# A hybrid attention block on one core: all engines in written order through the attention stages, score masks between normalisation steps, decay rows prepared amid the value projection

## The chip, the cores and the metric

The kernel runs on one core of a Trainium2 chip. The metric is device time in microseconds. The core's engines are TensorE (PE in the profile, with its weight loads as PEld), VectorE (DVE), ScalarE (ACT), GpSimd (POOL) and SyncE (SP), which here issues nearly all DMAs. Each engine takes its own instructions strictly in the order in which they stand; engines wait for each other on semaphores.

## The reference

One layer of a decoder block. Two attentions read the same normalised input, one with low-rank queries and keys (MLA), one with a forget gate (FoX); each has 16 heads of 64 and 512 tokens behind 16 learned ones. Their gated outputs are merged.

```python
u = rmsnorm(h, pre_norm_g[l])
proj = u @ w_in[l]
(cq, ckv, k_pe_raw, z_mla, fq, fk, fv, f_logit, z_fox, gate_a, gate_b) = jnp.split(proj, split_idx, axis=-1)
q = (rmsnorm(cq, mla_q_norm_g[l]) @ w_uq[l])...
kv = (rmsnorm(ckv, mla_kv_norm_g[l]) @ w_ukv[l])...
o_mla = causal_block_attention(q_m, k_m, v_mla, MLA_SCALE)
y_mla = (o_mla * jax.nn.silu(z_mla)) @ w_br_mla[l]
log_f = jax.nn.log_sigmoid((f_logit + fox_forget_b[l]).astype(jnp.float32)).transpose(0, 2, 1)
cum = jnp.cumsum(log_f, axis=-1)
o_fox = causal_block_attention(fox_heads(fq), fox_heads(fk), fox_heads(fv), FOX_SCALE, cum)
y_fox = (o_fox * jax.nn.silu(z_fox)) @ w_br_fox[l]
mixed = (jax.nn.sigmoid(gate_a) * y_mla + jax.nn.sigmoid(gate_b) * y_fox) @ w_out[l]
h = h + rmsnorm(mixed, post_norm_g[l])
```

In the FoX branch a logit gets `cum[t] - cum[s]`; the term of the query falls out of the softmax, so the kernel adds only a row over the keys.

## The kernel before

Float32 operands are split into a high and a low part, and a product is three matmuls (high by high, high by low, low by high). A weight tile is loaded as `wraw` (line 132, SP), cast to `wh` on ScalarE (line 141), and its rest `wl` is formed on GpSimd or VectorE (line 117).

After an opening, 16 attention stages run, one for each pair of heads and branch: `stages` takes FoX, then MLA, for pairs 0 to 7. A stage has these steps.

- Scores: `scores(0)` for query blocks 0 to 2, `scores(1)` for block 3. TensorE writes them to four rotating PSUM banks (`st`). VectorE adds the mask row, keeps the running minimum for the softmax (line 925), and so frees the bank. In MLA the row is `maskt`; in FoX it is `cdiag` (the decay with the causal mask in it) for the diagonal block, and for keys before it a copy of the plain decay in the last tile of `gT`.
- Exponentials (line 935, ScalarE), reciprocals of the sums (944, 945, VectorE), normalised probabilities as a high half (963, ScalarE) and a low half (964, VectorE), the 16 learned tokens' on GpSimd (950 to 955), and DMA transposes `pt<-pn` on SP (971), eight for a stage.
- `values()`: the product `ov` of a stage's probabilities and values. It is run one stage later, on TensorE between the two groups of scores.
- `fill`: the projections for the next stage and for the gates, between and behind the steps above. In a FoX stage these are `z` (both gates), MLA's `mq`, `mk` and `v`; in an MLA stage FoX's `fq`, `fk` and `v`, 48 matmuls each for `fk` and `v`. Pair 1's MLA stage also has the second half of the rotary queries (`ppe`). The keys' and queries' halves are written by `hl_done` (266 on ScalarE, 117 on VectorE). For `v` VectorE finds the peak of each half (805), then a power of two (810 to 815), and ScalarE scales (825).

A FoX stage's decay rows take three steps. `load_diag` brings `c_dram` into `cdiag`, a row of 528 numbers spread over 128 partitions for each of two heads (line 285, two DMAs). `keep_off` copies the part before the diagonal into `gT` (289, ScalarE). `mask_diag` adds the causal mask to `cdiag` in place (294, VectorE).

What sets the order: in the first stage every engine's instructions stand as the code is written. From the second on only TensorE's do; for the other four a scheduler orders them by priority, with `tc.high_priority` around masks, exponentials and casts. `load_diag` is called in an MLA stage and `keep_off` and `mask_diag` when `fk` is done, but the scheduler moves them, as the rows below show.

Of the kernel before, what the change touches and what calls it, by code (L numbers as in the profile page):

```python
# [14 lines left out]
BF16 = mybir.dt.bfloat16  # L15
# [8 lines left out]
S = 512  # L24
META = 16
# [29 lines left out]
def block_kernel(ctx: ExitStack, tc: tile.TileContext, x, meta_tokens, pre_norm_g, w_in, fox_forget_b,  # L55
# [238 lines left out]
        nc.vector.tensor_tensor(out=d, in0=d, in1=m, op=ALU.add)  # L294

    def k_fox(pr, put=None):
        halves = hl_done(("k", 1, pr), L, HALF, put)

        def done(i, ps):
            halves(i, ps)  # L300
            if pr and i:
                keep_off()
                mask_diag()
        return unit(f"fk{pr}", win_w(O_FK, pr), u_act, KD, ALLT, done)

# [360 lines left out]
    with ExitStack() as att:  # L668
# [45 lines left out]
        def q_mla(pr):  # L714
            kv = wukv.rearrange("p (h a e) -> p a h e", a=2, e=HD)

            def wrap(w):
                mw[pr] = w
                return (lambda k: w[k][0]), (lambda k: w[k][1])
            get = weights(lambda: [wuqh[:, k, 2 * pr : 2 * pr + 2, 0:NOPE] for k in range(2)]  # L720
                          + [kv[:, i, 2 * pr : 2 * pr + 2, :] for i in range(2)], wrap)

            halves = hl_done(("q", 0, pr), S, S)

            def q_done(i, ps):
                halves(i, ps)
                if pr:
                    load_qp(pr)
            return unit(f"mq{pr}", get, cq_act, 2, REAL, q_done)

# [142 lines left out]
        def attention(br, pr):  # L875
# [28 lines left out]
            def scores(g):  # L904

                banks = (((0, 0, 144, 0), (1, 0, 272, 144)), ((2, 0, 400, 0),)) if g == 0 else \
                    (((3, 0, HALF, 0),), ((3, HALF, L - HALF, 0),))

                def fn():
                    if g == 0:  # L910
                        for t in ("nb", "su", "ri"):
                            sums[t] = aw.tile([128, 2, 4], F32, tag=t, name=f"{t}{nm_}")
                    sfs[g] = aw.tile([128, 2, (2 * SF_STEP + 400, L)[g]], F32, tag=f"sf{g}", name=f"sf{nm_}{g}", bufs=1)
                    for ib, parts in enumerate(banks):
                        ps = [stp.tile([128, 512], F32, tag="st", name=f"st{nm_}{g}{ib}{h}") for h in range(2)]
                        for b, c0, w, o in parts:
                            for i, ops in enumerate(zip(*(sets(h, b, c0, w) for h in range(2)))):
                                for h, (Q, K) in enumerate(ops):
                                    mm(ps[h][:, o : o + w], Q, K, start=(i == 0), stop=(i == 4 - 2 * br))
                        for b, c0, w, o in parts:  # L920
                            for h in range(2):
                                nb = sums["nb"][:, h, b : b + 1]
                                for c1, n, add in terms(h, b, c0, w):
                                    with tc.high_priority(offset=100):
                                        nc.vector.tensor_tensor_reduce(  # L925
                                            out=sf_of(h, b)[:, c1 : c1 + n], in0=ps[h][:, o + c1 - c0 : o + c1 - c0 + n],
                                            in1=add, scale=-scale, scalar=3.0e38 if c1 == 0 else nb,
                                            op0=ALU.add, op1=ALU.min, accum_out=nb)

                def ex(mid={}):  # L930
                    with tc.high_priority(offset=60):
                        for b in GRP[g]:
                            for h in range(2):
                                sf = sf_of(h, b)
                                nc.scalar.activation(sf, sf, AF.Exp, bias=sums["nb"][:, h, b : b + 1], scale=-1.0,  # L935
                                                     accum_out=sums["su"][:, h, b : b + 1])
                                mid.get((b, h), int)()
                return fn, ex

            def norm(g):  # L940
                def fn(mid=int):
                    b0, nb_ = GRP[g][0], len(GRP[g])
                    su, ri = (sums[t][:, :, b0 : b0 + nb_] for t in ("su", "ri"))
                    nc.vector.tensor_scalar(out=su, in0=su, scalar1=1.0 / PSCALE, scalar2=None, op0=ALU.mult)
# [8 lines left out]
                    nc.gpsimd.tensor_copy(hi, mt)  # L953
                    nc.gpsimd.tensor_tensor(out=lo, in0=mt, in1=hi, op=ALU.subtract)
                    nc.gpsimd.tensor_copy(hi2, mt)
                    for b in GRP[g]:
                        for h in range(2):
                            sf = sf_of(h, b)[:, META:].rearrange("p (j c) -> p j c", c=128)
                            t0 = PN_STEP * (b % 3) + 1
                            hi, lo = (pn[g][:, h, t0 : t0 + 2 * b + 2].rearrange("p (j l) c -> p j l c", l=2)[:, :, i]  # L960
                                      for i in range(2))
                            rib = sums["ri"][:, h, b : b + 1]
                            nc.scalar.activation(hi, sf, AF.Copy, scale=rib)  # L963
                            nc.vector.scalar_tensor_tensor(out=lo, in0=sf, scalar=rib, in1=hi, op0=ALU.mult,  # L964
                                                           op1=ALU.subtract)
                    for b in GRP[g]:
                        if b == 1:
                            mid()
                        for h in range(2):
                            t0 = PN_STEP * (b % 3)  # L970
                            nc.sync.dma_start_transpose(
                                out=pts[h][:, 0 : 2 * b + 3, 128 * b : 128 * b + 128],
                                in_=pn[g][:, h, t0 : t0 + 2 * b + 3].rearrange("p t c -> p (t c)"))
                return fn

            def values():
                po = ovp.tile([128, 512], F32, tag="ov", name=f"ov{nm_}")
# [3 lines left out]
                for j in range(4):  # L981
                    for i, (v, p) in enumerate(((0, 0), (0, 1), (1, 0))):
                        for h in range(2):
                            mm(ph[h][:, 128 * j :], vps[br][:, j, h, v], pts[h][:, 1 + 2 * j + p, 128 * j :], start=False,
                               stop=(j == 3 and i == 2))
                nc.vector.scalar_tensor_tensor(out=gT[br][:, pr, :], in0=po, scalar=vsc[br, pr], in1=sils[br, pr],
                                               op0=ALU.mult, op1=ALU.mult)
                if br and pr % 2:
                    g2 = gT[1][:, pr - 1 : pr + 1].rearrange("p k s -> p (k s)")
                    sumsq(g2, gss[:, 1, pr // 2 : pr // 2 + 1], sils[1, pr].bitcast(BF16))  # L990

            return scores(0), scores(1), norm(0), norm(1), values

# [4 lines left out]
        def feed(br, pr):  # L998

            q = (q_mla, q_fox)[br](pr)  # L1000
            k = (k_mla, k_fox)[br](pr)
            v, vts[br, pr] = v_unit(br, pr, put=(br, pr) == (0, 0))
            return q, k, v

        def ahead(steps):
# [48 lines left out]
            for name in LAST:  # L1054
                later[name]()
        pe, pe_turn, pe_rest, _ = pe_unit(1)
        fills[3][25:25] = pe + [(0, pe_turn)] + [(0, lambda x=x: pe_rest(x)) for x in (1, 0)]
        steps = sum(fills[1:], []) + tail + mgates[0].steps
        ahead(steps)
        nxt = [fn for _, fn in steps if hasattr(fn, "load")]  # L1060
        late = []
        for si, (br, pr) in enumerate(stages):
            (s0, e0), (s1, e1), n0, n1, va = attention(br, pr)

            fill = fills[si]
            with ExitStack() as head:
                if si == 0:
                    head.enter_context(tc.manual_schedule(engines={E_.PE, E_.SP, E_.Pool, E_.Activation, E_.DVE}))
                    s0()
                    e0()  # L1070
                    run(fill[:3])
                    lo("b")()
                    nxt[1].load()
                    nxt[2].load()
                    n0()
                    s1()
                    run(fill[3:8])
                    e1()
                    run(fill[9:11])
                    run(fill[8:9])  # L1080
                    n1()
                    for x in (1, 0):
                        for i in range(2):
                            rope0[2](i, x, 2)
                    run(fill[11:18])
                    nxt[0].make()
                    run(fill[18:22])
                    for name in ("vr0", "vr1", "vs", "vz"):
                        later[name]()
                    nxt[1].make()  # L1090
                    run(fill[22:])
                    later["vT"]()
                    nxt[2].make()
                else:
                    s0()
                    e0()
                    for fn in late:
                        fn()
                    s1()
                    e1()  # L1100
                    if br == 0 and pr + 1 < NH // 2:
                        load_diag(pr + 1)
                    run(fill[:4])
                    n0()
                    run(fill[4:11])
                    n1()
                    run(fill[11:])
            late = [va]
        run(tail[:4])
        mgates[0].make()  # L1110
        for g in mgates[1:3]:
            g.load()
        va()
        run(tail[4:])


    fctx.close()
# [372 lines left out]
```

## Time and profile before

| | us |
|---|---|
| median of three runs | 621.31 (620.94 to 621.5) |
| the profiled execution | 621.72 |
| its span, first to last instruction | 619.9 |

The page gives the busy time of each engine over the span; the list of waits says for whom an engine stood idle, with the total, the count and the longest; a window gives busy times within a stretch; the timeline gives instructions in order of time, with the idle time before them in brackets. The granted clock of TensorE is 0.997 over the span.

### The profile page before, as it was taken

What the parts mean: (1) busy time and instruction counts of PE and PEld (TensorE: products, weight loads), DVE (VectorE), ACT (ScalarE), POOL (GpSimd) and SP (SyncE); (2) the same over time, 40 slices, a digit from 0 to 9 for tenths busy, and PEclk for the clock granted to TensorE, in tenths of its full rate; (3) what the DMA queues carried; (4) which work ended last, traced back from release to release, by engine and by line L of the source; (5) the groups of instructions that cost most, each with busy time, mean ns of one, the idle gap of its engine ahead of it and who ended that gap; (6) DMA issues with size and microseconds to landing.
All of it is one profiled execution on the core that took longest, in us unless ns stands there. A gap on an engine that the chain in (4) does not pass through costs nothing. (4 is left out here: it accounts for less than half of the span.)

```text
span 619.9 us, 11591 instructions
## 1 busy us (share of the span) xinstructions
PE 603.1 (97%) x3986; PEld 490.9 (79%) x3986; DVE 408.9 (66%) x1129; ACT 389.0 (63%) x855; POOL 176.5 (28%) x227
## 2 busy tenths in 40 slices
PE   9999969999999999999999999999999999999996
PEld 5889759879879879879779788787888875565885
DVE  5948755686675874884874874766977865556134
ACT  7756856676775874874794784776767654444421
POOL 2002444344653353444343353420000000003700
PEclk9999999999999999999999999999999999999999
DMA  9514569876777478476587666677252137332202
GB/s 305 127 39 133 145 149 182 182 178 158 213 153 182 127 170 181 104 180 161 146 161 144 164 152 156 127 176 219 62 152 83 35 88 251 102 106 100 102 35 102
DMA packets 206790, 88.85 MB, mean 143 GB/s; under 512 B 122858, under 2 KB 197994, under 8 KB 206731
## 3 DMA queue, kind: packets, MB, share of 16 engines
q1 hardware_dynamic: 206728, 88.11, 55.8%
q8 instruction: 31, 0.51, 0.3%
q14 instruction: 29, 0.23, 0.2%
q10 hardware_dynamic: 2, 0.00, 0.0%
HBM read 58.69 MB, written 3.97 MB: 101 GB/s over the span
## 5 line engine op out<-in xcount | busy, mean ns | idle before, releaser
L117 POOL TENSOR_TENSOR wl<-wraw,wh 128x1024 fp32r<-128x1024 f32 (+1 forms) x54 | 119.4, 2214 | 276.1 <-ACT wh L141 264.2
L141 ACT CAST wh<-wraw 128x1024 fp32r<-128x1024 f32 (+1 forms) x74 | 72.9, 987 | 83.9 <-issue 34.4
L935 ACT ACTIVATE sf<-sf,nb 128x272 f32<-128x272 f32 (+3 forms) x128 | 72.0, 570 | 10.4 <-DVE nb L925 10.3
L964 DVE SCALAR_TENSOR_TENSOR pn<-sf,ri,pn 128x128 f16<-128x128 f32 (+3 forms) x128 | 65.8, 554 | 2.9 <-ACT pn L963 2.5
L963 ACT ACTIVATE pn<-sf,ri 128x128 f16<-128x128 f32 (+3 forms) x128 | 61.8, 550 | 6.6 <-ACT sf L935 4.1
L91 PE MATMUL pg<-uTh,wh 128*128 128x512 f32 x128 | 51.9, 406 | 0.0
L91 PE MATMUL z<-uTh,wh 128*128 128x512 f32 x128 | 51.1, 400 | 0.0
L91 PE MATMUL z<-uTl,wh 128*128 128x512 f32 x128 | 50.1, 391 | 0.0
L91 PE MATMUL z<-uTh,wl 128*128 128x512 f32 x128 | 50.0, 391 | 0.0
L91 PE MATMUL pg<-uTh,wl 128*128 128x512 f32 x128 | 50.0, 391 | 0.0
L91 PE MATMUL pg<-uTl,wh 128*128 128x512 f32 x128 | 49.8, 389 | 0.0
L91 PE MATMUL st<-hlk,hlq 64*128 64x272 f32 (+3 forms) x480 | 47.8, 312 | 0.0
L91 PE MATMUL py<-g,yw 128*128 128x512 f16 x192 | 42.6, 379 | 0.6 <-DVE yw L1253 0.6
L91 PEld LDWEIGHTS st<-hlk,hlq 64*128 64x128 f32 x480 | 35.6, 188 | 7.2 <-issue 3.8
L91 PE MATMUL fk<-uTh,wh 128*128 128x256 f32 (+1 forms) x128 | 36.6, 286 | 0.0
L91 PE MATMUL v<-uTh,wh 128*128 128x256 f32 (+1 forms) x128 | 36.5, 285 | 0.0
L91 PE MATMUL fk<-uTh,wl 128*128 128x256 f32 (+1 forms) x128 | 36.5, 285 | 0.0
L91 PE MATMUL fk<-uTl,wh 128*128 128x256 f32 (+1 forms) x128 | 36.4, 285 | 0.0
L91 PE MATMUL v<-uTl,wh 128*128 128x256 f32 (+1 forms) x128 | 36.4, 285 | 0.0
L91 PE MATMUL v<-uTh,wl 128*128 128x256 f32 (+1 forms) x128 | 36.4, 285 | 0.0
L91 PEld LDWEIGHTS <-yw 128*128 128x128 f16 x192 | 17.9, 98 | 22.7 <-DVE yw L1253 1.1
L805 DVE TENSOR_REDUCE vsc<-v 128x1 f32<-128x272 f32 (+1 forms) x32 | 13.2, 433 | 33.3 <-PE v L91 33.3
(303 smaller groups left out, 1556.9 us busy)
## 6 DMA issues: line engine op xcount, KB each, us to landing
wraw<-in_w_in_dram SPq DMA_DIRECT2D x56, 512.0 KB, 3.6
cdiag<-c_dram SPq DMA_DIRECT2D x16, 264.0 KB, 4.8
yraw<-in_w_br_fox_dram SPq DMA_DIRECT2D x8, 512.0 KB, 3.8
yraw<-in_w_br_mla_dram SPq DMA_DIRECT2D x8, 512.0 KB
wraw<-in_w_out_dram SPq DMA_DIRECT2D x8, 512.0 KB, 4.8
pt<-pn SPq DMA_TRANSPOSE x128, 2.8
xr<-in_x_dram SPq DMA_DIRECT2D x4, 512.0 KB
out_dram<-yo SPq DMA_DIRECT2D x8, 256.0 KB, 2.1
```

The source lines that it names most:

```text
L91: nc.tensor.matmul(*a, **k)
L117: eng.tensor_tensor(out=lo, in0=src, in1=f32(hi), op=ALU.subtract)
L141: nc.scalar.copy(wh[:, :n], raw[:, :n])
L805: nc.vector.tensor_reduce(out=st["sc"][:, i : i + 1], in_=ps, op=ALU.max, axis=AX.X, apply_absolute_value=True)
L935: nc.scalar.activation(sf, sf, AF.Exp, bias=sums["nb"][:, h, b : b + 1], scale=-1.0, accum_out=sums["su"][:, h, b : b + 1])
L963: nc.scalar.activation(hi, sf, AF.Copy, scale=rib)
L964: nc.vector.scalar_tensor_tensor(out=lo, in0=sf, scalar=rib, in1=hi, op0=ALU.mult, op1=ALU.subtract)
```

## The change

All five engines now follow the written order through all 16 stages. TensorE's own order is the same, instruction by instruction. The score function is split in two, `products` (TensorE) and `masks` (VectorE, a few at a time); the normalisation in three, `sums_`, `halves` (one block and head) and `turn` (its transpose); `values()` returns its gating product and its squares, to be called later. Weight splits (`make`), the small steps of `v` and the decay rows are called by name.

```diff
-                def fn():
+                todo = []
+
+                def products():
...
-                                        nc.vector.tensor_tensor_reduce(
...
+                                    todo.append((h, b, c1, n, ps[h][:, o + c1 - c0 : o + c1 - c0 + n], add))
+
+                def masks(count=99):
+                    for h, b, c1, n, ps, add in todo[:count]:
+                        nb = sums["nb"][:, h, b : b + 1]
+                        nc.vector.tensor_tensor_reduce(
...
+                    del todo[:count]
```

The order of a stage behind the first, as it is written now:

```diff
-                    s0()
-                    e0()
-                    for fn in late:
-                        fn()
-                    s1()
-                    e1()
-                    if br == 0 and pr + 1 < NH // 2:
-                        load_diag(pr + 1)
-                    run(fill[:4])
-                    n0()
-                    run(fill[4:11])
-                    n1()
-                    run(fill[11:])
+                s0()
+                m0()
+                e0()
...
+                gated, squares = last()
+                last = values
+                s1()
+                n0()
+                gated()
+                for i, (h, b) in enumerate(first):
+                    h0(h, b)
+                    if i < 2:
+                        m1(2 + br)
+                    if h:
+                        t0(0, b)
+                        t0(1, b)
+                e1()
+                n1()
+                if br:
+                    second()
+                    run(fill[:8])
+                    make()
+                    squares()
+                    run(fill[8:22])
+                    small("vr0", "vr1", "vs", "vz")
+                    make()
+                    run(fill[22:])
+                    small("vT")
+                    make()
+                    continue
+                run(fill[:4])
+                second()
+                squares()
...
+                run(fill[4:9])
+                make()
+                load_qp(pr + 1)
+                load_diag(pr + 1)
+                run(fill[9:25])
+                make()
...
+                v = fill[-16:]
+                run(v[:8])
+                small("vr0")
+                keep_off()
+                mask_diag()
...
+                run(v[8:])
+                small("vr1", "vs", "vz", "vT")
+                make()
```

`k_fox` and `q_mla` lose their calls of `keep_off`, `mask_diag` and `load_qp`, and `v` is written with its small steps apart (`put=True`) in every stage.

First place: SP in the FoX stage of pair 3, before (`cdiag` the next pair's decay rows, `pt<-pn` the transposes):

```order
L132 DMA wraw_2817<-in_w_in_dram 128x8x128
L132 DMA wraw_2847<-in_w_in_dram 128x8x128
L285 DMA cdiag<-c_dram 128x528 x2
L971 DMA_TRANSPOSE pt_624<-pn_622 128x3x128
L971 DMA_TRANSPOSE pt_625<-pn_622 128x3x128
```

The load stands ahead of that stage's transposes; `QP`, MLA's rotary queries, is loaded after the first two transposes of the MLA stage.

SP in the MLA stage of pair 3, after the change:

```order
L960 DMA_TRANSPOSE pt_624<-pn_622 128x7x128
L960 DMA_TRANSPOSE pt_625<-pn_622 128x7x128
L960 DMA_TRANSPOSE pt_624<-pn_623 128x9x128
L960 DMA_TRANSPOSE pt_625<-pn_623 128x9x128
L132 DMA wraw_3121<-in_w_in_dram 128x8x128
L705 DMA QP<-qpe_dram 128x512
L285 DMA cdiag<-c_dram 128x528 x2
L132 DMA wraw_3185<-in_w_in_dram 128x8x128
```

Both loads now stand behind all eight transposes of the MLA stage and behind a weight load.

Second place: VectorE around the mask of the decay rows. Before, it stands in the FoX stage (pair 3), between the low half of MLA's queries and those of its keys:

```order
L117 TENSOR_TENSOR hlq_2826<-mq_2819,hlq_2826 128x512
L294 TENSOR_TENSOR cdiag<-cdiag,maskt 128x2x512
L117 TENSOR_TENSOR hlk_2869<-mk_2865,hlk_2869 128x272
L117 TENSOR_TENSOR hlk_2869<-mk_2872,hlk_2869 128x256
L805 TENSOR_REDUCE vsc_2888<-v_2884 128x1
```

After, it stands in the MLA stage of pair 3, between the peaks of the two halves of `v`; the first masks of the next FoX stage follow:

```order
L792 TENSOR_REDUCE vsc_3212<-v_3187 128x1
L294 TENSOR_TENSOR cdiag<-cdiag,maskt 128x2x512
L792 TENSOR_REDUCE vsc_3212<-v_3217 128x1
L797 TENSOR_SCALAR vsc_3212<-vsc_3212 128x1
L798 TENSOR_SCALAR vsc_3212<-vsc_3212 128x1
L800 TENSOR_SCALAR vsc_3212<-vsc_3212 128x1
L802 RECIPROCAL vsc_3212<-vsc_3212 128x1
L917 ISA sf_3260,nb_3257<-st_3261,cdiag 128x144
```

So everything that VectorE does for the next FoX stage now stands behind the mask, and the mask behind the load of `cdiag`.

More of the change, by code (lines that the diff above doesn't have):

```diff
@@ L296, in k_fox @@
     def k_fox(pr, put=None):
[L297 to L304, printed above, removed]
+        return unit(f"fk{pr}", win_w(O_FK, pr), u_act, KD, ALLT, hl_done(("k", 1, pr), L, HALF, put))
     gctx = [ExitStack(), ExitStack()]
@@ L721, in q_mla @@
                           + [kv[:, i, 2 * pr : 2 * pr + 2, :] for i in range(2)], wrap)
[L723 to L729, printed above, removed]
+            return unit(f"mq{pr}", get, cq_act, 2, REAL, hl_done(("q", 0, pr), S, S))
         def pe_unit(g, get0=None, put=None):
@@ L920, in fn @@
                         for b, c0, w, o in parts:
[L921 to L928, printed above, removed]
+                            for pair in zip(*(terms(h, b, c0, w) for h in range(2))):
+                                for h, (c1, n, add) in enumerate(pair):
+                                    todo.append((h, b, c1, n, ps[h][:, o + c1 - c0 : o + c1 - c0 + n], add))
[3 more added lines that the diff above has]
+                        nc.vector.tensor_tensor_reduce(
+                            out=sf_of(h, b)[:, c1 : c1 + n], in0=ps, in1=add, scale=-scale,
+                            scalar=3.0e38 if c1 == 0 else nb, op0=ALU.add, op1=ALU.min, accum_out=nb)
+                    del todo[:count]
                 def ex(mid={}):
@@ L937, in ex, with sums_ @@
                                 mid.get((b, h), int)()
-                return fn, ex
+                return products, masks, ex
             def norm(g):
-                def fn(mid=int):
+                def sums_():
                     b0, nb_ = GRP[g][0], len(GRP[g])
@@ L955, in fn, with halves, turn @@
                     nc.gpsimd.tensor_copy(hi2, mt)
[L956 to L974, printed above, removed]
+                def halves(h, b):
+                    sf = sf_of(h, b)[:, META:].rearrange("p (j c) -> p j c", c=128)
+                    t0 = PN_STEP * (b % 3) + 1
+                    hi, lo = (pn[g][:, h, t0 : t0 + 2 * b + 2].rearrange("p (j l) c -> p j l c", l=2)[:, :, i]
+                              for i in range(2))
+                    rib = sums["ri"][:, h, b : b + 1]
+                    nc.scalar.activation(hi, sf, AF.Copy, scale=rib)
+                    nc.vector.scalar_tensor_tensor(out=lo, in0=sf, scalar=rib, in1=hi, op0=ALU.mult, op1=ALU.subtract)
+                def turn(h, b):
+                    t0 = PN_STEP * (b % 3)
+                    nc.sync.dma_start_transpose(
+                        out=pts[h][:, 0 : 2 * b + 3, 128 * b : 128 * b + 128],
+                        in_=pn[g][:, h, t0 : t0 + 2 * b + 3].rearrange("p t c -> p (t c)"))
+                return sums_, halves, turn
             def values():
@@ L985, in values, with gated, squares @@
                                stop=(j == 3 and i == 2))
[L986 to L990, printed above, removed]
+                def gated():
+                    nc.vector.scalar_tensor_tensor(out=gT[br][:, pr, :], in0=po, scalar=vsc[br, pr], in1=sils[br, pr],
+                                                   op0=ALU.mult, op1=ALU.mult)
+                def squares():
+                    if br and pr % 2:
+                        g2 = gT[1][:, pr - 1 : pr + 1].rearrange("p k s -> p (k s)")
+                        sumsq(g2, gss[:, 1, pr // 2 : pr // 2 + 1], sils[1, pr].bitcast(BF16))
+                return gated, squares
             return scores(0), scores(1), norm(0), norm(1), values
@@ L1001, in feed @@
             k = (k_mla, k_fox)[br](pr)
-            v, vts[br, pr] = v_unit(br, pr, put=(br, pr) == (0, 0))
+            v, vts[br, pr] = v_unit(br, pr, put=True)
             return q, k, v
@@ L1056, in block_kernel @@
         pe, pe_turn, pe_rest, _ = pe_unit(1)
-        fills[3][25:25] = pe + [(0, pe_turn)] + [(0, lambda x=x: pe_rest(x)) for x in (1, 0)]
+        fills[3][25:25] = pe
         steps = sum(fills[1:], []) + tail + mgates[0].steps
@@ L1060, in block_kernel, with make, small, second @@
         nxt = [fn for _, fn in steps if hasattr(fn, "load")]
[L1061 to L1066, printed above, removed]
+        queue = nxt[3:-1]
+        def make():
+            queue.pop(0).make()
+        def small(*names):
+            for name in names:
+                later[name]()
+        with tc.manual_schedule(engines={E_.PE, E_.SP, E_.Pool, E_.Activation, E_.DVE}):
+            last = None
+            for si, (br, pr) in enumerate(stages):
+                (s0, m0, e0), (s1, m1, e1), (n0, h0, t0), (n1, h1, t1), values = attention(br, pr)
+                fill = fills[si]
+                first = [(h, b) for b in GRP[0] for h in range(2)]
+                def second():
+                    for h in range(2):
+                        h1(h, 3)
+                    for h in range(2):
+                        t1(h, 3)
+                s0()
+                m0()
+                e0()
                 if si == 0:
-                    head.enter_context(tc.manual_schedule(engines={E_.PE, E_.SP, E_.Pool, E_.Activation, E_.DVE}))
-                    s0()
-                    e0()
                     run(fill[:3])
@@ L1075, in block_kernel @@
                     n0()
+                    for h, b in first:
+                        h0(h, b)
+                    for h, b in first:
+                        t0(h, b)
                     s1()
+                    m1()
                     run(fill[3:8])
@@ L1087, in block_kernel @@
                     run(fill[18:22])
-                    for name in ("vr0", "vr1", "vs", "vz"):
-                        later[name]()
+                    small("vr0", "vr1", "vs", "vz")
                     nxt[1].make()
                     run(fill[22:])
-                    later["vT"]()
+                    small("vT")
                     nxt[2].make()
-                else:
-                    s0()
-                    e0()
-                    for fn in late:
-                        fn()
-                    s1()
-                    e1()
-                    if br == 0 and pr + 1 < NH // 2:
-                        load_diag(pr + 1)
-                    run(fill[:4])
-                    n0()
-                    run(fill[4:11])
-                    n1()
-                    run(fill[11:])
@@ L1108, in block_kernel @@
[L1108 to L1114, printed above, removed]
+                    last = values
+                    continue
+                gated, squares = last()
+                last = values
+                s1()
+                n0()
+                gated()
+                for i, (h, b) in enumerate(first):
+                    h0(h, b)
+                    if i < 2:
[3 more added lines that the diff above has]
+                        t0(1, b)
@@ new lines, in block_kernel @@
+                e1()
[6 more added lines that the diff above has]
+                    run(fill[8:22])
+                    small("vr0", "vr1", "vs", "vz")
+                    make()
+                    run(fill[22:])
+                    small("vT")
+                    make()
+                    continue
+                run(fill[:4])
+                second()
+                squares()
@@ new lines, in block_kernel @@
+                if si + 1 == len(stages):
+                    run(fill[4:])
+                    break
+                run(fill[4:9])
[4 more added lines that the diff above has]
+                make()
+                if si == 3:
+                    run(fill[25:29])
+                    pe_turn()
+                    make()
+                v = fill[-16:]
+                run(v[:8])
+                small("vr0")
@@ L1117, in block_kernel @@
+                keep_off()
+                mask_diag()
+                if si == 3:
+                    for x in (1, 0):
+                        pe_rest(x)
+                run(v[8:])
+                small("vr1", "vs", "vz", "vT")
+                make()
+            run(tail[:4])
+            mgates[0].make()
+            for g in mgates[1:3]:
+                g.load()
+            last()[0]()
+            run(tail[4:])
     fctx.close()
```

## The prediction

> **What bounds the kernel now.** First the page's head, then the list of waits on TensorE.
>
> ```profile
> span 619.9 us, 11591 instructions
> ...
> PE 603.1 (97%) x3986; PEld 490.9 (79%) x3986; DVE 408.9 (66%) x1129; ACT 389.0 (63%) x855; POOL 176.5 (28%) x227
> ```
> ```profile
> PE ov L91 <- DMA pt<-pn: 5.0, 4, 3.2
> PE v L91 <- DVE hlk L117: 4.1, 7, 1.0
> ```
> TensorE is busy for 97% of the span and its order is not changed, so the change can only win back its waits in the attention stages, or add new ones. Two waits are listed there: the values' product `ov` for its transposes (5.0), and the value projection `v` for the keys' lower halves (4.1). What they cost with all that hangs on them is read from stage lengths: windows that begin where a stage's scores begin, with length, busy time of PE, PEld, DVE, ACT, POOL, and PE's granted clock.
>
> ```profile
> 82.74:112.36 29.62, 25.80 (x203) 23.02 (x202) 14.19 (x45) 16.27 (x39) 11.71 (x14) 0.94 0.82 175
> ...
> 132.47:158.88 26.41, 26.41 (x215) 23.62 (x214) 15.62 (x48) 17.36 (x42) 15.74 (x18) 1.00 0.74 186
> ...
> 202.88:223.00 20.12, 19.59 (x129) 15.47 (x128) 17.43 (x60) 15.22 (x38) 7.39 (x11) 1.00 0.49 120
> 223.00:246.64 23.64, 23.64 (x203) 21.39 (x202) 13.17 (x44) 15.48 (x39) 10.70 (x13) 1.00 0.81 184
> ...
> 379.47:398.79 19.32, 19.32 (x128) 15.55 (x128) 14.84 (x59) 14.37 (x36) 7.37 (x11) 1.00 0.45 84
> ```
> The stages alternate: forgetting attention (I call it F), then MLA (M), for pairs 0 to 7. F3 takes 20.12; F7, whose `v` doesn't wait, takes 19.32. M3 takes 23.64 with PE never idle; M0 takes 29.62. So M0 has 5.98 to give, and F1 to F6 about 0.80 each.
>
> Why F waits is seen on four engines at one place of F3:
>
> ```profile
> 217.31 0.95 ACT L289 COPY gT<-cdiag 128x400 f32<-128x400 f32 x2
> 218.29 2.68 DVE L294 TENSOR_TENSOR cdiag<-cdiag,maskt 128x1024 f32<-128x1024 f32 x1 [0.73 <-ACT gT L289]
> 220.89 0.76 DVE L117 TENSOR_TENSOR hlk<-mk,hlk 128x272 fp32r<-128x272 f32 x2
> 221.38 0.40 PE L91 MATMUL v<-cTh,wh 128*128 128x272 f32 x1 [0.53 <-DVE hlk L117]
> 217.49 2.40 POOL L117 TENSOR_TENSOR wl<-wraw,wh 128x1024 fp32r<-128x1024 f32 x1 [4.62 <-ACT wh L141]
> ```
> VectorE adds the causal mask to the next pair's decay rows (`cdiag`) for 2.68, and the keys' lower half, for which PE waits, stands behind it. And in M0:
>
> ```profile
> 81.26 1.01 SPq L285 DMA_DIRECT2D cdiag<-c_dram  x2
> 82.37 4.86 SPq L971 DMA_TRANSPOSE pt<-pn  x2
> 87.29 3.65 SPq L784 DMA_DIRECT2D qpe_dram<-gT  x4
> ...
> 86.44 0.52 ACT L289 COPY gT<-cdiag 128x400 f32<-128x400 f32 x1 [5.08 <-DMA cdiag<-c_dram]
> ...
> 87.67 1.22 DVE L294 TENSOR_TENSOR cdiag<-cdiag,maskt 128x1024 f32<-128x1024 f32 x1 [5.09 <-ACT gT L289]
> ...
> 88.27 0.38 PE L91 MATMUL ov<-pt,vm 80*64 80x512 f16 x1 [3.17 <-DMA pt<-pn]
> ```
> The load of `cdiag` goes ahead of F0's last two transposes, ScalarE and VectorE stand for 5 us until it lands, and PE waits 3.17 for the transposes.
>
> **What the change removes.** (1) In M0 the load no longer stands there, so the transposes follow from 81.26 at about 1.24 each; the second lands some 2.8 after its issue at 82.5, thus at 85.3, where `ov` asks at 85.0. I leave 0.3 and take 5.7. (2) In F1 to F6 the mask leaves the place ahead of the keys: 6 x 0.80 = 4.8. (3) The other waits of `ov` are 5.0 less M0's 3.17 and 0.61, that is 1.2. ScalarE now writes probabilities right after the first group's exponentials, not after the second's, so transposes start earlier in F and this goes. Together 11.7. F0's wait at `v` (the 1.0 of the list) stays, since F0 was in written order already.
>
> **What it adds.** The two copies and the mask now stand in M, on VectorE between the peaks of the two halves of `v`, and the load of `cdiag` stands on SP behind M's eight transposes, one weight load and the load of `QP`. In M3, from its start at 223.00:
>
> ```profile
> 223.06 0.53 SPq L132 DMA_DIRECT2D wraw<-in_w_in_dram  x1
> 225.89 1.82 SPq L132 DMA_DIRECT2D wraw<-in_w_uq_dram  x2
> 227.76 0.97 SPq L132 DMA_DIRECT2D wraw<-in_w_ukv_dram  x2
> 228.83 0.41 SPq L132 DMA_DIRECT2D wraw<-in_w_in_dram  x1
> 230.52 2.48 SPq L971 DMA_TRANSPOSE pt<-pn  x2
> 233.09 0.53 SPq L712 DMA_DIRECT2D QP<-qpe_dram  x1
> 233.71 8.65 SPq L971 DMA_TRANSPOSE pt<-pn  x6
> 242.45 1.16 SPq L132 DMA_DIRECT2D wraw<-in_w_in_dram  x2
> ```
> ```profile
> 230.08 0.41 POOL L954 TENSOR_TENSOR pn<-mt,pn 128x96 f16<-128x96 f32 x1
> ```
> ```profile
> L971 SPq DMA_TRANSPOSE pt<-pn x128: 1178/1237/3468, 71.8 to 416.4; - x128
> ```
> ```profile
> DMA to landing us min/median/max: 4.2/4.8/5.2
> ```
> The first transpose goes at 7.5 into the stage, when GpSimd's last piece is there; the work ahead of it (masks, exponentials) keeps its order in M, so it can't go earlier. Eight issues take 2.48 + 8.65; without `QP` between them they end at 18.7. Then a weight load (0.63 with its gap), `QP` (0.62), and the two loads of `cdiag`, the second at 20.4. The last row is that of `cdiag`'s loads (min, median, max): with 4.8 it lands at 25.2. A copy of 0.52 and the mask at 1.22 end at 27.0. VectorE wants to go on earlier:
>
> ```profile
> 243.88 0.44 DVE L805 TENSOR_REDUCE vsc<-v 128x1 f32<-128x272 f32 x1 [1.70 <-PE v L91]
> 246.75 0.42 DVE L805 TENSOR_REDUCE vsc<-v 128x1 f32<-128x256 f32 x1 [2.43 <-PE v L91]
> ```
> The second peak was due at 246.75, 23.75 into the stage. It comes **3.3 late**, and behind it on VectorE stand the scale of `v` and all score masks of the next F. Those free the score banks:
>
> ```profile
> 206.64 0.35 DVE L925 CUSTOM_DVE_ANT_0 sf<-st,cdiag,nb 128x128 f32<-128x128 f32 x1
> ...
> 206.30 1.38 PE L91 MATMUL st<-hlk,hlq 64*128 64x272 f32 x12
> ```
> In F3 the last mask of the first group ended at 206.92, while PE was within the second group's scores, whose last bank takes that buffer. There is no slack, so PE waits about as long as VectorE is late, in each F from F1 to F7.
>
> The sum: F3 to F7 5 x 3.3 = 16.5. M1 is 26.41 long, 2.77 more than M3, since it holds the second half of the rotary queries, so F2 waits only 0.5. In M0 SP still has four stores (3.65) and the weight loads (0.53 + 1.82 + 0.97 + 0.41 in M3) between F0's transposes, which end near 83.8, and its own; with gaps of 0.4 these start at 91.6, 8.8 into the stage, 1.2 later than in M3: 4.5 for F1. **Added: 21.5.** Against the profiled execution's own 621.72 (span 619.9 and 1.8 around it): 621.72 - 11.7 + 21.5 = 631.5. The median of the runs is 621.31, 0.4 lower, so **631**.
>
> Bounds of the lateness. Low: landing 4.2, and eight transposes at the least 1.18, 1.7 less in all, make 1.0; the added waits are 5 x 1.0 + 2.2 = 7.2, which gives 617. High: landing 5.2 and a mask of 2.68 make 5.2; 5 x 5.2 + 6.4 + 2.4 = 34.8 gives 645. I take 3.3, the row's medians.
>
> At nothing I cost the following. Masks between normalisation steps on VectorE: the banks they free are next taken by the transposition of `v`, 24 matmuls of 512 columns after the scores; if that cover is gone, PE waits for as long as the masks outlast it. The gating product behind the reciprocal: 0.7 later, read only by later stages. The load of `QP` 10 us later: wanted a stage of about 20 us on. The peaks, scales and casts written out one by one are the same instructions.
>
> **Two rules of the skill.** The mask took 2.68 where GpSimd was in a weight split (217.49 to 219.89) and 1.22 at 87.67 with GpSimd idle.
>
> ```profile
> 241.53 1.29 POOL L117 TENSOR_TENSOR wl<-wraw,wh 128x512 fp32r<-128x512 f32 x1 [1.75 <-ACT wh L141]
> ```
> In M the split nearest the mask's new place ends at 242.82, 19.8 into the stage, before the mask starts at 25.8, so I use 1.22. The Trainium skill (SBUF — State Buffer, Who interferes with whom) says that a VectorE instruction with two SBUF inputs and a GpSimd one that reads SBUF exclude each other for the whole instruction. The two rows agree; by the rule a collision would add about 1.46 in each F, 10 in all.
>
> ```profile
> wraw<-in_w_in_dram SPq DMA_DIRECT2D x56, 512.0 KB, 3.6
> ```
> A weight load issued at 18.7 lands at 22.3 by this row, and `cdiag` is issued at 20.0 behind it. If `cdiag` moves only then, its 4.8 end at 27.1, 1.9 later than I took, or 11 over six stages. The Trainium skill (DMA: Bandwidth & Descriptors, Queues, rings and completion order) says that each DMA engine consumes descriptors in ring order, which would put it that way; no row here shows `cdiag` behind a weight load.
>
> **The rivals.**
> *The cover holds* (faster). If the second `cdiag` load were issued by about 17.1, it would land by 21.9 and the mask would end by 23.75: nothing is added and 621.3 - 11.7 = 610. It needs SP to be 3.3 ahead of my count. For it: the transposes' data are ready earlier than SP issues them. Against: SP issues eight in a row at its own pace in the rows above. Chance 0.18.
> *Half of it* (even). Lateness 1.9 in five stages, 2.7 in F1, nothing in F2 add 12, as much as is removed: 618 to 623. It needs SP at its least pace. Chance 0.15.
> *More than late.* The collision of 1.46, `cdiag` behind the weight load, or PE's clock:
>
> ```profile
> 90.00:92.00 2.00, 2.00 (x21) 1.68 (x17) 2.00 (x12) 2.00 (x6) 2.00 (x2) 0.54 0.38 121
> ```
> After M0's waits the granted clock was 0.54 in these 2 us: of M0's 5.98, 3.8 are waits and 2.2 come of the clock, which after six waits of 3.3 would be 13. Any one gives 641 to 645. Chance 0.12.
> *My forecast*, 623 to 638: 0.55.
>
> **Numbers.** A measurement of this kernel can tell about 0.2% (1.2 us) from no change. Faster takes the first rival and half of the second: 0.26; same 0.07; slower 0.67. The range 609 to 638 leaves out most of the third rival and a little of the first, about 0.15. As over a quarter lies on the other side, the likeliest case's own range is 623 to 638.
>
> **What would show it.** In the changed kernel's waits a new line of PE `st` for VectorE, about 20 us in seven or more pieces; ScalarE idle before its copies of `cdiag` for a DMA; the mask at 1.2, late in M. F stages near 22.6, M stages at 23.64, M0 near 24. PE's waits of `v` for `hlk` down to F0's 1.0. I am wrong if `cdiag` is issued before 18 into the stage, if it lands in under 4, or if F stages are 19.3.

## The result, and the profile after

The changed kernel takes 663.28 us (661.24 to 664.07, four runs) beside 621.12 for the kernel before: a ratio of 1.067, with a 95% interval of 1.065 to 1.070. It is slower, as forecast, but by 42 us where 10 were forecast, and outside the range of 609 to 638. The profiled execution took 661.24, 39.5 more than that of before.

The page's head and TensorE's list of waits (total, count, longest):

```profile
span 659.4 us, 11566 instructions
...
PE 616.7 (94%) x3986; PEld 501.0 (76%) x3986; DVE 398.2 (60%) x1129; ACT 390.9 (59%) x855; POOL 179.5 (27%) x227
```
```profile
PE st L91 <- DVE nb L917: 30.3, 10, 9.1
PE ov L91 <- DMA pt<-pn: 1.3, 3, 0.7
PE v L91 <- DVE hlk L117: 1.2, 1, 1.2
...
PE pg L91 <- DVE wl L117: 0.7, 1, 0.7
PE mk L91 <- DVE hlq L117: 0.7, 1, 0.7
```

The waits at `v` and `ov` went as forecast, and the forecast line is there: TensorE waits 30.3 for score masks. But TensorE is also 13.6 busier with the same 3986 matmuls. The windows by stage, with the same columns as in the prediction, are those of M0, F1, F2, F3, M3 and F7:

```profile
82.95:107.18 24.23, 23.95 (x202) 21.69 (x201) 13.11 (x44) 14.66 (x37) 11.71 (x14) 1.00 0.70 158
107.18:139.24 32.06, 22.53 (x130) 18.02 (x129) 15.86 (x60) 15.54 (x38) 7.52 (x11) 0.84 0.67 151
...
165.63:186.56 20.93, 19.88 (x130) 15.79 (x129) 15.47 (x60) 15.14 (x38) 10.52 (x13) 1.00 0.89 170
...
210.14:237.25 27.11, 22.57 (x129) 17.90 (x128) 15.88 (x60) 15.64 (x38) 7.55 (x11) 0.87 0.55 136
237.25:260.88 23.63, 23.63 (x204) 21.37 (x203) 13.00 (x44) 15.48 (x39) 10.65 (x13) 1.00 0.64 141
...
411.19:436.33 25.14, 21.36 (x128) 16.84 (x127) 15.85 (x60) 15.53 (x38) 7.54 (x11) 0.93 0.53 119
```

M0 is 5.4 shorter and M3 unchanged, as forecast. F3 is 27.11, not 22.6. Its granted clock is 0.87 over the stage; the column before the last two shows where, in stretches of F3:

```profile
213.00:217.00 4.00, 0.63 (x14) 0.47 (x10) 2.82 (x11) 1.29 (x4) 0.21 (x1) 1.00 0.20 59
217.00:218.00 1.00, 0.21 (x1) 0.18 (x1) 1.00 (x9) 1.00 (x2) 0.00 (x0) 1.00 0.00 0
218.00:219.00 1.00, 0.68 (x6) 0.42 (x5) 1.00 (x7) 1.00 (x6) 0.68 (x1) 0.82 0.00 0
219.00:225.00 6.00, 5.94 (x17) 4.78 (x18) 3.84 (x20) 5.21 (x16) 2.88 (x5) 0.50 0.39 107
```

TensorE stands still from 213.6 to 217.8 and then runs at half clock for some 7 us. The chain ahead of it, on the timelines of SP, ScalarE and VectorE:

```profile
194.08 11.45 SPq L960 DMA_TRANSPOSE pt<-pn  x8
205.63 0.53 SPq L132 DMA_DIRECT2D wraw<-in_w_in_dram  x1
206.25 0.53 SPq L705 DMA_DIRECT2D QP<-qpe_dram  x1
206.84 0.90 SPq L285 DMA_DIRECT2D cdiag<-c_dram  x2
```
```profile
213.48 0.52 ACT L289 COPY gT<-cdiag 128x400 f32<-128x400 f32 x1 [0.26 <-DMA cdiag<-c_dram]
...
214.04 1.22 DVE L294 TENSOR_TENSOR cdiag<-cdiag,maskt 128x1024 f32<-128x1024 f32 x1 [6.22 <-ACT gT L289]
...
217.79 0.88 PE L91 MATMUL st<-hlk,hlq 64*128 64x272 f32 x6 [4.16 <-DVE nb L917]
```
```profile
DMA to landing us min/median/max: 5.4/6.0/6.6
```

M2 began at 186.56, so the transposes begin 7.5 into the stage, the second load of `cdiag` is issued at 20.75, and it lands near 26.9. The last row is for `cdiag`: a median of 6.0, where I took the 4.8 of before. The mask took 1.22.

Where the 39.5 came from, from stage starts in both traces: F1 to F7 are 44.7 longer together, M0 is 5.4 shorter, M1 to M6 2.0 shorter, what follows F7 2.0 longer (why stays open), and the head 0.2. Of F's 44.7, 30.3 are waits at `st`, and 17.5 are what is left of F1 and F3 to F7 beyond the 19.3 of an undisturbed stage and their waits (3.2, 3.3, 2.4, 3.4, 3.3, 2.0). Most of this is half clock, but not all: where masks are late and the clock stays at 1.00, TensorE is busy for 19.8 to 20.0 a stage all the same (19.88 in F2 above, 20.01 in F3 of experiment 2, 19.76 in F7 of experiment 5). So the half clock itself cost some 13 to 15. The 4.8 of the old waits at `v` went out; F2's 1.2 beyond its wait at `st`, and a wait of 0.4 at `ov` in F1, make up the rest.

### The profile page after: what moved, and what is told of

It is laid out like the page before. It is cut to its first block, busy times and chain, and to the rows that moved or that the text cites. A ratio compares the mean times of both kernels' runs of the same rounds, so it can differ in the third digit from the quotient of the medians.

```text
span 659.4 us, 11566 instructions
## 1 busy us (share of the span) xinstructions
PE 616.7 (94%) x3986; PEld 501.0 (76%) x3986; DVE 398.2 (60%) x1129; ACT 390.9 (59%) x855; POOL 179.5 (27%) x227
## 5 line engine op out<-in xcount | busy, mean ns | idle before, releaser
L91 PE MATMUL st<-hlk,hlq 64*128 64x272 f32 (+3 forms) x480 | 52.8, 326 | 30.3 <-DVE nb L917 30.3
L927 ACT ACTIVATE sf<-sf,nb 128x144 f32<-128x144 f32 (+3 forms) x128 | 72.1, 570 | 4.3 <-DVE nb L917 4.2
L91 PEld LDWEIGHTS st<-hlk,hlq 64*128 64x128 f32 x480 | 39.3, 197 | 38.7 <-issue 33.3
L91 PE MATMUL z<-uTh,wh 128*128 128x512 f32 x128 | 56.3, 440 | 0.0
L91 PE MATMUL z<-uTl,wh 128*128 128x512 f32 x128 | 54.4, 425 | 0.0
L91 PE MATMUL z<-uTh,wl 128*128 128x512 f32 x128 | 53.8, 420 | 0.0
L289 ACT COPY gT<-cdiag 128x400 f32<-128x400 f32 x16 | 8.3, 524 | 54.5 <-DMA cdiag<-c_dram 54.3
L294 DVE TENSOR_TENSOR cdiag<-cdiag,maskt 128x1024 f32<-128x1024 f32 x8 | 9.9, 1234 | 46.1 <-ACT gT L289 46.1
```

The costliest lines, as they stand in the source:

```text
L91: nc.tensor.matmul(*a, **k)
L289: nc.scalar.copy(gT[h][:, KD - 1, 0:OFF], cdiag[:, h, 0:OFF])
```

## The experiments

Diffs are against the kernel after, unless another is named. A time without a ratio is that of a single run.

**1. The load early** (`e1_early_load`).

```diff
+                if br == 0 and si + 1 < len(stages):
+                    load_diag(pr + 1)
                 gated, squares = last()
...
                 load_qp(pr + 1)
-                load_diag(pr + 1)
```

> The kernel after, with the load of cdiag alone moved: it stands ahead of the MLA stage's transposes, not behind them, the weight load and QP. Theory (the late load of cdiag makes the waits, and the half clock follows from them): PE no longer waits at st, the granted clock is 1.00 in F1 to F7, these are 19.3 to 19.6 long, and 661.2 becomes 612 (609 to 615). Rival (masks taken in turns with the normalisation, or the mask's place between the two peaks, hold up the score banks): waits at st stay, F stages stay above 21, and the time above 625.

It took 620.09, a ratio of 0.997 (0.996 to 0.999) to the kernel before. Moving this one load takes 43 us off. TensorE's waits and the stage F3:

```profile
PE mk L91 <- DVE hlq L117: 4.1, 6, 0.8
PE ov L91 <- DMA pt<-pn: 2.8, 4, 1.1
PE v L91 <- DVE hlk L117: 1.2, 1, 1.2
```
```profile
198.55:218.85 20.30, 19.66 (x129) 15.61 (x128) 14.73 (x59) 14.52 (x36) 7.55 (x11) 1.00 0.53 118
```

There is no wait at `st`, and the clock is 1.00. The late load made both, so the rival falls. But 612 was missed by 8: F2 to F6 are 20.3, no better than before. Each has a new wait of 0.64 to 0.68 at `mk` for the queries' lower half, where before there was one at `v` for the keys'; F7, with 0.82 at `mk`, is 1.2 longer than before. The waits of M0's and M7's transposes are 1.1 and 1.0. In the kernel after, which has one wait of 0.67 at `mk` and two of 0.40 and 0.66 for those transposes, the lateness covered most of this.

**2. The load ahead of the weight load and `QP`, 3. behind the weight load, ahead of `QP`, and 4. behind six transposes** (`e2_ahead_of_weight`, `e8_behind_weight`, `e9_behind_six`): the same call at three places of the MLA stage. Ahead of both:

```diff
                 run(fill[4:9])
+                load_diag(pr + 1)
                 make()
                 load_qp(pr + 1)
-                load_diag(pr + 1)
```

Behind the weight load:

```diff
                 make()
+                load_diag(pr + 1)
                 load_qp(pr + 1)
-                load_diag(pr + 1)
```

Behind six transposes (`second` issues the last two):

```diff
                 run(fill[:4])
+                if si + 1 < len(stages):
+                    load_diag(pr + 1)
                 second()
...
                 load_qp(pr + 1)
-                load_diag(pr + 1)
```

> The kernel after, with the load of cdiag still behind all eight transposes, but ahead of the weight load and of QP. Theory (cdiag lands late because it moves behind the weight load and QP): its second load goes 1.1 earlier and lands in 4.8, not 6.0, so 2.3 earlier in all; PE's waits at st in F3 to F7 go from 3.4-4.8 to 1.1-2.5, the clock stays 1.00 there, and the time is 633 (628 to 638). Rival (cdiag takes 6.0 wherever it stands, from what else moves in this stage): waits near 3.0, the half clock still follows some of them, time 645 to 652.

> The kernel after, with the load of cdiag ahead of QP but still behind the weight load. Theory (each load ahead of cdiag in SP's queue adds to its landing): the second issue goes 0.6 earlier; landing between the 6.0 of the kernel after and the 5.0 of the load ahead of both: near 6.0 if the weight load (512 KB) makes the difference, near 5.0 if QP does. Waits of 2.5 to 4 in F3 to F7, 650 to 659. No rival on the time; the landing decides.

> The kernel after, with the load of cdiag behind six of the eight transposes. Theory (a second load that is issued by about 17.1 into the MLA stage costs nothing): issue 3.9 earlier, landing 5.0, so 4.9 earlier in all; no wait at st in F2 to F7, the clock 1.00, these 20.3 long as with the early load; F1 keeps about 4.2 and a half clock of 3; 626 (623 to 629). Rival (two transposes behind the load come late): waits at ov for pt in F2 to F7, 0.5 to 1.5 each, 630 to 636.

Ahead of both, it took 644.97 (ratio 1.036, 1.032 to 1.039), between my range and the rival's. `cdiag` landed after 5.0 (its row stands first among the three below), and the waits of F3 to F7 (with the second, of 0.3 to 0.4) fell to 1.5 to 3.1, near what the theory gave. The clock is what I had wrong. F3 and F4 of this kernel:

```profile
205.91:229.01 23.10, 20.01 (x128) 15.79 (x128) 15.86 (x60) 15.37 (x38) 7.52 (x11) 1.00 0.63 151
252.60:277.64 25.04, 22.62 (x129) 17.82 (x129) 15.85 (x60) 15.12 (x37) 7.54 (x11) 0.86 0.59 145
```

F3 waited 2.03 and 0.39 for masks, F4 2.15 and 0.26. F4's matmuls are busy for 2.6 more, at a clock of 0.86. So the same waits cost nothing more in one stage and about 2 us more in the next; the last section shows what differs.

Behind the weight load, 656.75. The rows of `cdiag`'s landing are that of the load ahead of both, that of this run, and that of the run behind six transposes:

```profile
DMA to landing us min/median/max: 5.0/5.0/5.1
```
```profile
DMA to landing us min/median/max: 4.9/5.1/6.6
```
```profile
DMA to landing us min/median/max: 4.5/4.6/5.9
```

With the weight load ahead of it, `cdiag` took 5.1; with the weight load behind it, 5.0; with `QP` ahead as well, 6.0. So `QP` cost about 0.9, and the weight load next to nothing. Experiments 5, 6 and 7, which leave the load where the kernel after has it, have medians of 5.9, 5.7 and 6.0. The time lay in the range, with waits of 2.5 to 3.9.

Behind six transposes, 625.06: no wait at `st`, and F2 and F4 to F7 are 20.3 with a clock of 1.00. The bound of the prediction's first rival, that a load issued by about 17.1 costs nothing, agrees: in M2 the second load was issued at 16.8. F1 is 25.18, not through the 4.2 at `st` that I expected: the loads stood ahead of M0's last two transposes, `ov` waited 2.94 and 0.70 for them, much as in M0 before the change, and 3.4 us of half clock followed.

**5. The mask last** (`e3_mask_last`).

```diff
 small("vr0")
-keep_off()
-mask_diag()
...
 small("vr1", "vs", "vz", "vT")
+keep_off()
+mask_diag()
 make()
```

> The kernel after, with the copies of cdiag and its mask behind the second peak and the scale of v, not ahead of them; the load is as late as before. Theory (the chain load, copy, mask, score masks sets the wait): 1.1 less at each wait (0.42 + 0.21 + 3 x 0.16 for the peak and scale and their gaps), so 3.0 in F3, 2.3 in F7, 8.0 in F1; by the waits alone 655, and where a wait falls under about 3.2 the half clock goes too, down to 645. Rival (the scale of v, late behind the mask, holds the banks that PE wants next): the waits at st stay, z or vt wait less, time 655 to 661.

657.14: waits of 8.3 in F1 and 2.4 to 3.9 in F3 to F7, 0.2 to 1.0 less rather than 1.1, and F2 waited 2.4 where it had waited 0.4, since the second half of the rotary queries now stood ahead of the mask. I had expected the half clock to go where a wait falls under 3.2, and that isn't so: it came after 2.44 in F2 and 2.80 in F5, and not after 2.44 in F7. The time lies in the rival's range, but its sign, waits at `st` that stay, is only partly there. The place of the mask among the small steps of `v` is a minor term; a sharp reading isn't possible from one run.

**6. TensorE kept busy** (`e4_busy_pe`).

```diff
+if br and si > 4:
+    spare = acc(f"spare{si}")
+    for _ in range(16):
+        mm(spare, ALL1, ALL1.unsqueeze(1).broadcast_to([128, 4, 128]), start=True, stop=True)
 s1()
```

> The kernel after, with 16 matmuls of 512 columns added on TensorE in F3 to F7 between ov and the second group of scores, whose results nothing reads (about 3.4 us). Theory (PE's idle time itself brings the half clock): PE waits 0.3 to 1.4 in place of 3.4 to 4.8, the granted clock is 1.00 in F3 to F7, and 14 go: 647 (644 to 651), though more is computed. Rival (the clock is lowered for another reason than the wait): half clock stays, time 659 to 664.

657.49, so the forecast of 647 missed. F3, F4 and F7:

```profile
210.91:236.46 25.55, 23.57 (x145) 17.26 (x144) 15.86 (x60) 15.57 (x38) 7.52 (x11) 1.00 0.55 128
260.05:287.06 27.01, 24.89 (x145) 18.34 (x144) 15.86 (x60) 15.54 (x38) 7.54 (x11) 0.94 0.50 124
407.21:433.20 25.99, 24.91 (x145) 18.35 (x144) 15.86 (x60) 15.53 (x38) 7.54 (x11) 0.93 0.52 130
```

In F3 (and F5 and F6) the clock stayed at 1.00, and the stage is 1.6 to 2.3 shorter than without the extra matmuls, though it holds 3.6 us more of them. In F4 and F7 half clock came all the same, for about 3.4 us, in F7 behind waits of only 0.69 and 0.39:

```profile
410.63 3.63 PE L91 MATMUL spare<-ALL 128*128 128x512 bf16 x16
414.95 0.88 PE L91 MATMUL st<-hlk,hlq 64*128 64x272 f32 x6 [0.69 <-DVE nb L917]
416.22 0.86 PE L91 MATMUL st<-hlk,hlq 64*128 64x256 f32 x6 [0.39 <-DVE nb L917]
```

So less idle time took the half clock away in three stages, but the length of a wait alone doesn't decide. TensorE's wait for a score bank also ended 0.3, 1.3 and 0.8 later into F3, F4 and F7 than in the kernel after, and 0.3 earlier into F6, which this run doesn't explain.

**7. `z` inside the wait** (`e7_z_in_the_wait`).

```diff
+if br:
+    run(fill[:8])
 s1()
...
 second()
-run(fill[:8])
 make()
```

> The kernel after, cdiag as late as there, but in the FoX stages TensorE does the 24 matmuls of z (5.5 us) ahead of the second group of scores. Theory (the lateness costs only what PE has to stand still for): the waits of 3.4 to 4.8 in F3 to F7 are covered, the clock stays 1.00 there, F1 keeps 3 to 4 of its 9.1, and the time is 626 (622 to 632). Rival (the late masks hold up more than the score banks, such as the transposes that the next ov waits for): waits appear at ov or vt in place of st, and the time is above 640.

661.99, as slow as the kernel after:

```profile
PE vt L94 <- DVE nb L917: 25.6, 7, 4.3
PE mk L91 <- DVE hlq L117: 5.1, 5, 2.4
PE st L91 <- DVE nb L917: 3.6, 2, 3.2
```

The wait moved by one block. Behind the second scores TensorE transposes `v` into one of the same banks, and the 24 matmuls of `z` had been what covered the masks there. The rival was right: VectorE is late with more than the score banks, and `z` can cover one of the two places, not both. That no other work of TensorE could be put there isn't shown.

**8. Masks before the normalisation** (`e6_masks_first`; against experiment 1).

```diff
+m1()
 for i, (h, b) in enumerate(first):
     h0(h, b)
-    if i < 2:
-        m1(2 + br)
```

> The early load of cdiag, and the masks of the second group all ahead of the normalised low halves, not in turns with them. Theory (the banks that the masks free are wanted late, so their place among the halves costs nothing either way): within 1.5 of the 620.1 of the early load alone, no wait at st. Rival (turns matter): either PE waits for transposes at ov, which go 2 to 3 later, and it is 2 to 8 slower, or the exponentials of the second group start earlier and it is 2 faster.

621.36, a ratio of 1.000 (0.998 to 1.001) to the kernel before, 1.3 above experiment 1, whose interval (0.996 to 0.999) overlaps. The turns of masks and normalisation, which the title names, are worth 1 to 2 us at most, if anything.

**9. The cast later** (`e5_cast_later`; against experiment 1).

```diff
 second()
 run(fill[:8])
-make()
 squares()
-run(fill[8:22])
+run(fill[8:12])
+make()
+run(fill[12:22])
```

> The early load of cdiag, and in the FoX stages the next weight's cast (make) four steps later: on ScalarE behind the casts of vp, vm and the queries' upper half, not ahead of them. Theory (the 0.67 that PE waits for at mk in each FoX stage is new in the written order and comes of that cast, 1.04 on ScalarE ahead of the chain vp, vm, hlq): the waits at mk go, F2 to F7 fall from 20.3 to 19.3-19.7, and 620.1 becomes 616 (614.5 to 618). Rival (VectorE's low halves of the probabilities, in turns with the masks, make hlq late): mk still waits, the time stays at 619 to 621.

616.96, a ratio of 0.993 (0.991 to 0.996): 0.7% faster than the kernel before, and by the ratios 2.4 us faster than experiment 1. ScalarE in experiment 1, and F3 in this one:

```profile
212.16 1.04 ACT L141 CAST wh<-wraw 128x1024 fp32r<-128x1024 f32 x1
213.10 0.58 ACT L837 CAST vp<-vt 128x512 f16<-128x512 f32 x1
213.57 0.52 ACT L847 CAST vm<-vm 16x128 f16<-16x128 f32 x2
214.12 0.59 ACT L266 CAST hlq<-mq 128x512 fp32r<-128x512 f32 x1
```
```profile
197.93:217.64 19.71, 19.65 (x130) 15.61 (x129) 14.74 (x59) 14.54 (x36) 7.55 (x11) 1.00 0.51 124
```

A cast of 1.04 for a weight that can come four steps later stood ahead of the queries' halves. With it behind them F3 falls from 20.30 to 19.71, the wait at `mk` is gone in F2 to F6, and 0.26 are left in F7.

## Why the prediction was wrong in size

The mechanism held: the load of `cdiag` is late behind M's transposes, the mask and all score masks are late behind it, and TensorE waits at `st`, which experiment 1 shows by undoing that alone. Two steps of the sum failed: it put the half clock behind those waits at nothing, and it had `cdiag` land too early, by 1.2 in the median stage (4.8 taken, 6.0 measured) and by some 3 more in M0, whose transposes began later than it counted. Point by point:

- *Issue at 20.4 into the stage*: 20.75. *Mask at 1.22 without a collision*: 1.22, and GpSimd's split was over by then.
- *Landing at 4.8*: **6.0**. This is the step "with 4.8 it lands at 25.2". The row was that of a load with no `QP` ahead of it, and `QP` is what adds most of the 1.2 (experiments 2 and 3). I had thought of an extra from the queue, laid it to the weight load, and left it to a rival. The rule that I drew from the Trainium skill (DMA: Bandwidth & Descriptors, Queues, rings and completion order) would have put `cdiag` behind the weight load whole. No run here shows that: the prediction's count of it is 1.9 more, and experiment 3 has 0.1 more.
- *3.3 in each of F3 to F7*: 3.8 to 4.7, 20.8 together instead of 16.5. This is the landing, less what slack there was.
- *4.5 in F1*: **9.1**. I took M3's issue times for M0's weight loads (3.7). In M0 they last from 87.92 to 94.87, so its transposes begin 12.1 into the stage, not 8.8:

```profile
88.44 3.36 SPq L132 DMA_DIRECT2D wraw<-in_w_uq_dram  x2
91.85 2.49 SPq L132 DMA_DIRECT2D wraw<-in_w_ukv_dram  x2
94.44 0.43 SPq L132 DMA_DIRECT2D wraw<-in_w_in_dram  x1
95.05 12.77 SPq L960 DMA_TRANSPOSE pt<-pn  x8
```

  M0's own rows in the trace of before were as slow, and I should have used them:

```profile
92.05 2.75 SPq L132 DMA_DIRECT2D wraw<-in_w_uq_dram  x2
94.85 2.19 SPq L132 DMA_DIRECT2D wraw<-in_w_ukv_dram  x2
```

  Why these issues are slow there wasn't tried.
- *The clock*: counted at nothing in the forecast and at 13 in a rival that I gave 0.12; it is **13 to 15** of the 17.5 above, the largest error, and about the rival's price. I had the row (0.54 after a wait of 3.17 in M0) and the price (2.2, which is somewhat high: M0's 3.4 us at half clock can cost 1.7), yet left it out of a sum whose waits were said to be 3.3. Beyond that, I took the rival's three causes one at a time, "any one gives 641 to 645", while the clock and the longer landing came together.
- *5.7 from M0*: 5.4. *1.2 from other waits of `ov`*: M5, which had waited 0.80, is 1.2 shorter, and M2 and M4 are 0.4 shorter each, but 1.06 come back as waits for M0's and M7's transposes.
- *4.8 from F1 to F6*: the wait at `v` went, but experiment 1 shows that it wasn't to be had by this order: a new wait at `mk` takes its place. I had cast the order of the casts aside as "the same instructions". With it mended, 19.7 a stage.

Added up: 631.5, with 4.6 more in F1, 4.3 in F3 to F7, 17.5 for the clock and what comes with it, and 2.0 behind F7, is 659.9, beside 661.24 measured.

## What to carry to other kernels

A load that is moved behind a row of transfers on its queue must be counted to its landing with the queue as it will then be, not with the old median, and stage by stage with that stage's own rows. When a busy TensorE is to get waits of some microseconds, price the half clock behind them from the trace's own example, and add up the parts of a bad case that have one cause. In an order written by hand, look for the instruction with the latest user that stands ahead of one with the earliest: here the place of two DMA issues of 0.4 us was worth 43 us, and that of a cast of 1 us another 2 to 3.

## What the runs showed of the hardware

The half clock came in pieces of 3.41 us (F7 of the kernel after, after a wait of 3.40; M0 of before, after 3.17), of 6.8 (F3, after 4.16) or of 10.2 (F1), on and off at once between 1.00 and 0.50. These are one, two and three times 3.41. A window's mean clock tells when it switched within it: these pairs give 90.18 to 93.59 in M0 of before, and 258.86 to 265.68 in F4 of experiment 2.

```profile
90.00:90.25 0.25, 0.25 (x6) 0.19 (x4) 0.25 (x2) 0.25 (x2) 0.25 (x1) 0.86 0.39 115
93.50:93.75 0.25, 0.25 (x8) 0.25 (x8) 0.00 (x0) 0.25 (x3) 0.25 (x1) 0.82 1.19 295
```
```profile
258.50:259.00 0.50, 0.50 (x6) 0.86 0.00 0
265.50:266.00 0.50, 0.50 (x3) 0.82 0.19 33
```

What decides is not the wait's length alone: after 2.15 and 0.26 it came, after 2.03 and 0.39 not (experiment 2); after 2.44 and 0.39 it came in F2 of experiment 5 and stayed away in F7. The switches lie on a fixed grid. In the kernel after, half clock sets in at 116.23, 218.63, 266.42, 317.62, 368.82 and 420.02, and these are apart by 30, 14, 15, 15 and 15 times 3.413; the five other traces with more than one piece have such a grid too, each at an offset of its own. What counts is how busy TensorE is within one step of it. In the attention stages of the eight traces that have half clock there, each of the 29 steps at full clock with TensorE busy for at most 41% was followed by a step at half clock; of the 12 with 43 to 54%, 3 were; and of the 781 busier ones, one (68%, F7 of experiment 6, which stays open). The wait of F4 in experiment 2 lies whole within a step, which was busy for 37%; that of F3 is parted by the grid, and its step was busy for 51%. So where a wait falls on the grid is luck, and half clock behind a given wait can be priced only as an average. This is read from traces; no run was made to move the grid.

The Trainium skill (TensorE: Matmul & The Clock Gate, What's actually happening) says that the clock falls after one or more idle windows of about 3.4 us, and that the window is free-running. The length and the fixed grid agree; that the window has to be idle doesn't, since steps with TensorE busy for up to 41% sufficed.

That `QP` lengthens the landing of the load behind it by about 0.9 and the weight load, twice as large, by 0.1 was not expected either, and stays unexplained.
